# Layer 2's output projection: low weight parts formed by accumulating transfers in twelve units

## The chip, the core and the metric

The kernel runs on one core of a Trainium2 chip. The metric is the device time of the core in microseconds (us), the median of three executions: 2115.39 us for the kernel before (2115.34 to 2115.5). Beside it stands one execution taken by the hardware profiler; every duration of a single instruction below comes from that one.

## The reference

Two layers are computed over 512 tokens of width 2048 in float32: a retention layer and a layer of latent attention (16 heads of width 128). Layer 2 ends in an output projection, and that is the place of the change:

```python
o = causal_block_attention(q, k, v).reshape(B, S, MLA_WIDTH)   # 512 x 2048
return (jax.nn.silu(g) * o) @ w_out                            # w_out: 2048 x 2048
# then: x = x + gate * y, and a final rmsnorm(x, final_norm_g)
```

## The kernel before

**Precision.** A float32 matrix product is made of three products of rounded parts. Every operand `a` is held as a high part (`a` rounded to TensorE's float32r format) and a low part (`a` minus the high part). `mm3` (lines 156 to 160) issues, for one block, high times high (L158), high times low (L159) and low times high (L160), always in this order; in the projection the weights' high part is the left operand of the first two, and the weights' low part that of the third.

**The two parts of a weight.** `load_w` (L138) makes one unit of weights ready: SP (SyncE's queue of transfers) loads 128 partitions x 1024 float32 (512 KB) from HBM into a tile `raw` (three such buffers); `split` (L134) has ScalarE (ACT) copy it, rounded, into the high part (L135), and VectorE (DVE) subtract that from `raw` into the low part (L136). High and low part lie side by side in one "pair" tile. There are three pair tiles, taken in turn (`next_pair`), so a unit cannot be split before the TensorE (PE) products of the unit that held its pair before have ended.

**The output projection.** Its 2048 output rows are made in four parts of 512. The first two parts (`r` = 0 and 1 in the loop at the end of the kernel) run through `chunk`: 8 units each, every unit with 2 x 128 rows of the inner dimension. I call the units of the first part A0 to A7 and those of the second B0 to B7; in the trace all their weights are named `o_w`, their raw tiles `o_w_raw`. One unit is 24 products of 128x512 on PE. The moving operand (`o_h`, `o_l`) is the gated attention output, fetched from HBM (`o_in`<-`o_d`) and split once, and kept. Parts three and four go another way (`seven_rows_steps` with the tiles `o_00e`, `o_00o`, ...; then `last_product`), and they draw from the same pair tiles: while B7 is prepared, `seven[0]` takes one pair of the rotation for `o_00o`. So B7's pair is the one that B5 held, two units before it, where the other units' pairs were held three units before.

**Beside it.** During A0 to A3 the last two attention heads (14 and 15) are finished; POOL (GpSimd) stores their output to HBM with plain transfers (L2137, 256 KB each), and `o_in` of A7 is loaded after those stores. During B2 to B5 DVE and ACT form sums for the third part (L2416 to L2419 and L135/L136 on tiles `o_s`, `o_t`).

**Order.** Every engine works through its instructions in one fixed order, which a scheduler writes when the program is built: `queued` and `behind` keep the order of the code for the engines that they name, and elsewhere priorities decide. A wait at the head of an engine's order holds all that is behind it.

Of the kernel before, what the change touches and what calls it, by code (L numbers as in the profile page):

```python
# [9 lines left out]
F32 = mybir.dt.float32  # L10
F32R = mybir.dt.float32r
I32 = mybir.dt.int32
AF = mybir.ActivationFunctionType
ALU = mybir.AluOpType
AX = mybir.AxisListType

P = 128
T = 512
# [31 lines left out]
def hybrid_trunk_kernel(  # L50
# [25 lines left out]
    nc = tc.nc  # L76
    PE, ACT, DVE, POOL = nc.tensor, nc.scalar, nc.vector, nc.gpsimd
# [3 lines left out]
    w_mla_in, w_uq, w_ukv, w_mla_out = mla_w_in[0], mla_w_uq[0], mla_w_ukv[0], mla_w_out[0]  # L81

    base = ctx.enter_context(tc.tile_pool(name="base", bufs=1))
# [50 lines left out]
    def split(src, hi, lo):  # L134
        ACT.copy(hi, src)  # L135
        DVE.tensor_sub(lo, src, hi.bitcast(F32))  # L136

    def load_w(parts, a, b, name, later=None, where=None, halved=False):  # L138

        raw = base.tile([P, a, b], F32, tag="raw", bufs=3, name=f"{name}_raw")  # L140
        for dst, src in parts:
            nc.sync.dma_start(dst(raw), src)
        hi, lo = two_tiles(where, [P, a, b], name, ASIDE if halved else EVEN)
        if later is None:
            split(raw, hi, lo)
        else:
            later.append(lambda: split(raw, hi, lo))
        return hi, lo

    def rows(w, u, n, c0, cn):  # L150
        return w[u * n * P : (u + 1) * n * P, c0 : c0 + cn].rearrange("(k p) n -> p k n", p=P)
# [79 lines left out]
    def next_pair(name):  # L231
        i = n_pairs[0] % 3
        n_pairs[0] += 1
        return ready.pop(i, None) or pair_tile(base, f"pair{i}", name)

    def parts_of(pair, shape, at):

        n = math.prod(shape[1:])
        views = [pair[:, 1024 * i + at : 1024 * i + at + n] for i in range(2)]
        return views if len(shape) == 2 else [v.rearrange("p (k n) -> p k n", k=shape[1]) for v in views]  # L240

    def two_tiles(where, shape, name, at=EVEN):

        if where is None:
            return parts_of(next_pair(name), shape, at)
        if callable(where):
            return parts_of(where(name), shape, at)
        return [base.tile(list(shape), F32R, tag=t, bufs=n, name=f"{name}_{i}") for i, (t, n) in enumerate(where)]
# [2118 lines left out]
    def scored(pieces):  # L2367
        scores, exps, normalise = pieces[:3]
        pieces[5]()
        for i in range(NT):  # L2370
            scores(i)
            exps(i)
        normalise()
# [27 lines left out]
    def o2_parts(u):  # L2401
        o2_in[u] = k4(f"o2_in{u}", F32)
        nc.sync.dma_start(o2_in[u], o2_d[u * 2 * P : (u + 1) * 2 * P, :].rearrange("(k p) n -> p k n", p=P))
        own = k4b if u < 2 else big
        o2_hl[u] = own(f"o2_h{u}"), own(f"o2_l{u}")
        split(o2_in[u], *o2_hl[u])
# [49 lines left out]
    with behind(V_):  # L2456
        scored(last[0])

    def o2_unit(r, u):
        with ExitStack() as stack:  # L2460
            for ins in o2_first if (r, u) in ((0, 1), (0, 2)) else ():
                stack.enter_context(tc.issue_after(ins))
            wt = load_w([(whole, rows(w_mla_out, u, 2, r * T, T))], 2, T, f"o2_w{r}_{u}")
        if u not in o2_hl:
            o2_parts(u)
        return wt
# [73 lines left out]
    for r in range(2):  # L2540
        run(
            chunk(
                [(lambda u=u: o2_unit(r, u), [2 * u, 2 * u + 1]) for u in range(KD // 2)],
                [(acc, aux)[r](f"o2_{r}_{b}") for b in range(4)],
                lambda w, ki, kt, b: w_block(w, ki, b), lambda w, ki, kt, b: o2_moving(kt),
                lambda b, ps: o2_out(b, ps)() if r == 0 else waiting.append(lambda: o2_out(4 + b, ps)()),
            ),
            each=lambda i: o2_hooks(r * (KD // 2) + i),
        )
# [236 lines left out]
```

## Time and profile before

| | us |
|---|---|
| Median of three executions | 2115.39 |
| Profiled execution, its own time | 2114.73 |
| Span of its instructions | 2113.0 |
| PE busy in the span | 2098.4 (99%) |
| DVE busy | 1680.8 (80%) |
| ACT busy | 1054.1 (50%) |
| POOL busy | 103.8 (5%) |

Times of the trace count from the span's start. A0's first product stands at 1920 us, B7's last ends at 2017 us, so the change touches a stretch of about 97 us. A row of the timeline gives the start, the duration, the engine, the line, the operation, and output<-input; an entry in square brackets is idle time before it and what ended it. "Landing" of a transfer is counted from its issue. Matmuls are pipelined: their rows last 0.39 us, but they follow each other every 0.23 us.

### The profile page before, as it was taken

How to read it: one execution, taken by the hardware profiler on the slowest of the kernel's cores; microseconds unless marked ns; L12 is line 12 of the kernel's file. 1: busy time of each engine (PE TensorE's matmuls, PEld its weight loads, DVE VectorE, ACT ScalarE, POOL GpSimd, SP SyncE). 2: the span in 40 equal slices, each digit the busy share in tenths (PEclk: the TensorE clock that was granted, in tenths of full speed). 3: DMA queues.
4: the chain of work that ended last, by engine and by line, in shares of the span. 5: the costliest groups of instructions: out<-in, count | busy, mean ns of one | idle time of the engine just before them, and what ended most of it. 6: DMA issues, size and time to landing. Idle time of an engine off the chain costs nothing.

```text
span 2113.0 us, 30423 instructions
## 1 busy us (share of the span) xinstructions
PE 2098.4 (99%) x11268; PEld 1814.2 (86%) x11268; DVE 1680.8 (80%) x2562; ACT 1054.1 (50%) x1626; POOL 103.8 (5%) x177
## 2 busy tenths in 40 slices
PE   8999999999999999999999999999999999999998
PEld 6888898989889888888888888898889999888898
DVE  7999888888888789666777877767978788887675
ACT  6765444444444444434344445345446565665343
POOL 1001010000000000000000000010000000000000
PEclk9999999999999999999999999999999999999999
DMA  9975786868777778755656656753556655455453
GB/s 382 407 281 195 250 276 222 278 216 268 245 259 250 237 237 278 260 188 183 234 170 227 220 184 235 265 178 111 167 186 207 199 166 187 153 188 176 148 166 126
DMA packets 237303, 465.08 MB, mean 220 GB/s; under 512 B 21169, under 2 KB 91857, under 8 KB 233569
## 3 DMA queue, kind: packets, MB, share of 16 engines
q1 hardware_dynamic: 224512, 423.17, 60.5%
q0 software_dynamic: 11920, 38.91, 4.8%
q8 instruction: 88, 1.44, 0.3%
q10 hardware_dynamic: 722, 1.06, 0.2%
q14 instruction: 61, 0.50, 0.1%
HBM read 420.06 MB, written 43.00 MB: 219 GB/s over the span
## 4 chain that ended last, share of the span: by engine, by line
PE 95%; DMA 3%; DVE 1%; ACT 0%; SPq 0%; issue 0%; POOLq 0%; DVEq 0%
PE o L1486 16%; PE x L884 2%; PE x L883 2%; PE y L884 2%; PE y L883 2%; PE s L884 2%; PE s L883 2%; PE x L885 2%; PE s L885 2%; PE y L885 2%; PE o L2607 2%; PE qk L158 2%; PE s_qk L984 2%; PE x_qk L984 2%; PE qk L160 2%; PE qk L159 2%
## 5 line engine op out<-in xcount | busy, mean ns | idle before, releaser
L1486 PE MATMUL o<-o_h,o_p 128*128 128x512 f32 (+1 forms) x1088 | 322.9, 377 | 0.0
L1486 PEld LDWEIGHTS o<-o_h,o_p 128*128 128x128 f32 x1088 | 200.2, 188 | 37.1
L1486 PE MATMUL o<-o_l,o_p 128*128 128x512 f32 (+1 forms) x544 | 204.8, 377 | 0.0
L136 DVE TENSOR_TENSOR o_p<-o_r,o_p 128x1024 fp32r<-128x1024 f32 x64 | 78.1, 1221 | 52.5 <-ACT o_p L135 52.2
L1486 PEld LDWEIGHTS o<-o_l,o_p 128*128 128x128 f32 x544 | 102.3, 188 | 18.2
L1170 DVE SCALAR_TENSOR_TENSOR mod<-mod,c_odd 128x1024 f32<-128x1024 f32 x56 | 67.2, 1219 | 14.9 <-DMA mod<-in_ada_t_dram 14.9
L135 ACT CAST o_p<-o_r 128x1024 fp32r<-128x1024 f32 x64 | 66.7, 1053 | 21.3 <-PE o L1486 7.7
L158 PE MATMUL qk<-hT,qk_p 128*128 128x512 f32 x192 | 75.0, 391 | 0.0
L160 PE MATMUL qk<-hT,qk_p 128*128 128x512 f32 x192 | 74.8, 390 | 0.0
L159 PE MATMUL qk<-hT,qk_p 128*128 128x512 f32 x192 | 74.7, 389 | 0.0
L389 DVE SCALAR_TENSOR_TENSOR aw<-aw,c_all 128x2048 f32<-128x2048 f32 (+1 forms) x37 | 73.2, 1997 | 1.6 <-DMA aw<-in_ada_t_dram 1.4
L1332 ACT ACTIVATE yn<-y,nmr,gn_r 128x512 f32<-128x512 f32 x32 | 22.3, 777 | 67.7 <-DVE nmr L1326 67.7
L159 PE MATMUL o<-o_l,o_w 128*128 128x512 f32 x128 | 49.9, 390 | 0.3 <-DVE o_l L136 0.3
L158 PE MATMUL o<-o_h,o_w 128*128 128x512 f32 x128 | 50.1, 391 | 0.0
L160 PE MATMUL o<-o_h,o_w 128*128 128x512 f32 x128 | 49.9, 390 | 0.0
L1170 DVE SCALAR_TENSOR_TENSOR mod<-mod,c_bm 128x1024 f32<-128x1024 f32 x40 | 48.7, 1218 | 0.0
L448 PE MATMUL g<-hT,g_p 128*128 128x512 f32 x192 | 46.1, 389 | 0.0
L2046 PE MATMUL uv<-ukv_p,kvT 128*128 128x256 f32 x384 | 46.1, 279 | 0.0
L136 DVE TENSOR_TENSOR qk_p<-qk_r,qk_p 128x1024 fp32r<-128x1024 f32 x23 | 27.9, 1222 | 22.1 <-ACT qk_p L135 21.8
L2046 PEld LDWEIGHTS uv<-ukv_p,kvT 128*128 128x128 f32 x384 | 44.9, 189 | 0.1
L2607 PE MATMUL o<-o_h,o_w 128*128 128x256 f32 (+1 forms) x208 | 43.6, 306 | 0.0
L160 PEld LDWEIGHTS qk<-hT,qk_p 128*128 128x128 f32 x192 | 36.0, 188 | 7.8 <-DVE qk_p L136 0.3
(1735 smaller groups left out, 6308.0 us busy)
## 6 DMA issues: line engine op xcount, KB each, us to landing
mod<-in_ada_t_dram SPq DMA_DIRECT2D x96, 512.0 KB, 5.7
o_r<-in_ret_w_out_dram SPq DMA_DIRECT2D x64, 512.0 KB, 5.4
aw<-in_ada_t_dram SPq DMA_DIRECT2D x28, 1024.0 KB, 9.5
mod_gate<-in_ada_t_dram SPq DMA_DIRECT2D x32, 512.0 KB, 5.1
qk_r<-in_ret_w_in_dram SPq DMA_DIRECT2D x48, 256.0 KB, 3.2
qk_r<-qk_d SPq DMA_DIRECT2D x32, 256.0 KB, 5.9
v_r<-v_d SPq DMA_DIRECT2D x32, 256.0 KB, 5.8
sg<-g_d SPq DMA_DIRECT2D x32, 256.0 KB, 6.2
```

What stands on the lines that cost most here:

```text
L136: DVE.tensor_sub(lo, src, hi.bitcast(F32))
L158: PE.matmul(o, lhs[0], rhs[0], start=first and not seeded, stop=False, skip_group_check=seeded)
L159: PE.matmul(o, lhs[0], rhs[1], start=False, stop=False, skip_group_check=seeded)
L160: return PE.matmul(o, lhs[1], rhs[0], start=False, stop=last, skip_group_check=seeded)
L883: PE.matmul(banks[b], a[0], w[0], start=first, stop=False, skip_group_check=True)
L884: PE.matmul(banks[b], a[0], w[1], start=False, stop=False, skip_group_check=True)
L885: PE.matmul(banks[b], a[1], w[0], start=False, stop=True, skip_group_check=True)
L984: PE.matmul(o, w[wp][:, i, b * P : (b + 1) * P], a[ap], start=first and i + b + k == 0, stop=k == 2, skip_group_check=True,)
L1170: DVE.scalar_tensor_tensor(out=aw, in0=aw, scalar=1.0, in1=silu_c[j], op0=ALU.mult, op1=ALU.mult, accum_out=row_sums[piece][:, j, b : b + 1],)
L1486: PE.matmul(o, w[i][:, ki, c0 + b * P : c0 + (b + 1) * P], a[j], start=first and i + j == 0, stop=last and i == 1, skip_group_check=True,)
L2046: PE.matmul(ps[:, (t % 2) * 256 : (t % 2 + 1) * 256], a[i], w[k], start=t % 2 + i + k == 0 and kt == 1, stop=kt == 3 and i == 1, skip_grou ...
L2607: PE.matmul(banks3[b][:, cols], last_w[u][i][:, ki, b * P : (b + 1) * P], o2_moving(2 * u + ki, cols)[j], start=u + ki + i + j == 0, stop= ...
```

## The change

In the units with `u` > 1, six in each of the two parts, `load_w` is replaced by a new function. DVE's subtraction is gone. ACT copies the high part as before, then writes the negated high part into the low part's tile; then POOL issues a transfer that reads the same weights from HBM a second time and adds them, in the transfer, to what lies in the tile. The low part is weights minus high part again. The units A0, A1, B0 and B1 stay as they were.

```diff
+    def load_remainder(src, name):
+
+        raw = base.tile([P, 2, T], F32, tag="raw", bufs=3, name=f"{name}_raw")
+        nc.sync.dma_start(raw, src)
+        hi, lo = two_tiles(None, [P, 2, T], name)
+        ACT.copy(hi, raw)
+        ACT.activation(lo, hi.bitcast(F32), AF.Identity, scale=-1.0)
+        POOL.dma_start(lo, src, accum_op=ALU.add)
+        return hi, lo
+
     def o2_unit(r, u):
         with ExitStack() as stack:
             for ins in o2_first if (r, u) in ((0, 1), (0, 2)) else ():
                 stack.enter_context(tc.issue_after(ins))
-            wt = load_w([(whole, rows(w_mla_out, u, 2, r * T, T))], 2, T, f"o2_w{r}_{u}")
+            if u > 1:
+                wt = load_remainder(rows(w_mla_out, u, 2, r * T, T), f"o2_w{r}_{u}")
+            else:
+                wt = load_w([(whole, rows(w_mla_out, u, 2, r * T, T))], 2, T, f"o2_w{r}_{u}")
```

The raw tile is now read by ACT's copy alone, and comes free after it. PE's order of products is the same. Two places show what moves. The first is ACT's order around the last units, B5 to B7 (`o_w_5` to `o_w_7`; L2464 is the copy, L2465 the negation, L1017 and L1022 are copies for the third part; the last number of a name is a buffer's):

```order
+L2464 CAST o_w_5_18497<-o_w_5_raw 128x1024
+L135 CAST o_s_18486<-o_s7f 128x2x256
+L2465 ACTIVATE o_w_5_18497<-o_w_5_18497 128x1024
+L2464 CAST o_w_6_18541<-o_w_6_raw 128x1024
+L2465 ACTIVATE o_w_6_18541<-o_w_6_18541 128x1024
 L1017 CAST o_2_00e<-o_2_00e_r 128x1024
 L1022 CAST o_2_00o<-o_2_00o_r 128x1024
-L135 CAST o_w_7_18575<-o_w_7_raw 128x1024
+L2464 CAST o_w_7_18586<-o_w_7_raw 128x1024
+L2465 ACTIVATE o_w_7_18586<-o_w_7_18586 128x1024
 L1017 CAST o_2_01e<-o_2_01e_r 128x1024
 L1022 CAST o_2_01o<-o_2_01o_r 128x1024
```

Each unit now has two ACT instructions where it had one, the second right behind the first or one instruction later. The second place is POOL's order, from the last stores of the attention heads through A2 to A7 (`o_w_2` to `o_w_7`):

```order
 L2137 DMA o_d<-o_13_17756 128x512
-L2137 DMA o_d<-o_14_17999 128x512
-L2137 DMA o_d<-o_15_18072 128x512
+L2466 DMA o_w_2_17953<-in_mla_w_out_dram 128x2x512
+L2466 DMA o_w_3_18027<-in_mla_w_out_dram 128x2x512
+L2466 DMA o_w_4_18079<-in_mla_w_out_dram 128x2x512
+L2466 DMA o_w_5_18119<-in_mla_w_out_dram 128x2x512
+L2137 DMA o_d<-o_14_18000 128x512
+L2466 DMA o_w_6_18167<-in_mla_w_out_dram 128x2x512
+L2137 DMA o_d<-o_15_18074 128x512
+L2466 DMA o_w_7_18215<-in_mla_w_out_dram 128x2x512
```

The stores of heads 14 and 15 now stand behind the accumulating transfers of A2 to A5, and of A6.

## The prediction

> **What bounds the kernel now.** I read the page's busy times first, then who waited for whom on PE, then the stretch of B2 to B7 (B for the second part's units, A for the first's), then its rows one by one. The page:
>
> ```profile
> PE 2098.4 (99%) x11268; PEld 1814.2 (86%) x11268; DVE 1680.8 (80%) x2562; ACT 1054.1 (50%) x1626; POOL 103.8 (5%) x177
> ```
>
> PE is the bound. Next the waits of PE from 1915 to 2060 us (who <- for whom: us, times, longest), and the busy time by engine from 1970 to 2017 us, that is A7's end to B7's:
>
> ```profile
> PE o L159 <- DVE o_l L136: 0.3, 1, 0.3
> ...
> 1970.00:2017.00 47.00, 47.00 (x209) 38.92 (x208) 32.80 (x55) 18.72 (x25) 0.00 (x0) 1.00 0.46 146
> ```
>
> PE lost 0.3 us in the whole neighbourhood of the change, in A0, which the change leaves as it is; in the B units it is busy 47.00 of 47.00 us. DVE, which is relieved, ends no wait of PE there. So nothing is to be gained, and the question is whether the low parts come later than PE's L160 asks for them.
>
> **The change part by part.** Here are the weights' own rows, and two ACT groups that bear on the new negation:
>
> ```profile
> L135 ACT CAST o_w<-o_w_raw x16: 1035/1051/1057, 1885.0 to 2008.4; 128x1024 fp32r<-128x1024 f32 x16
> L136 DVE TENSOR_TENSOR o_w<-o_w_raw,o_w x16: 1209/1224/1226, 1886.1 to 2009.5; 128x1024 fp32r<-128x1024 f32 x16
> ...
> L2485 ACT ACTIVATE x<-x,vcol 128x512 f32<-128x512 f32 x4 | 2.9, 722 | 0.1
> L2484 ACT ACTIVATE x_sq<-x 128x512 f32<-128x512 f32 x3 | 1.9, 617 | 0.0
> ```
>
> Removed: 12 subtractions of 1.22 us = 14.7 us of DVE, worth 0 on PE by the waits above. Added on ACT: 12 negations of 128x1024. ACT is busy 18.72 of 47.00 us in the B stretch, so the 6 of them there fit. The copy of the same size takes 1.05 us; the scaled activation of half the size takes 0.72 against 0.62 us for an unscaled one, so the negation takes 1.05 to 1.15 us. I take 1.1.
>
> Added on POOL: 12 issues, and on the DMA engines 12 x 512 KB read from HBM once more. The trace holds no accumulating transfer. The nearest rows, in the stretch from 1915 to 2020 us (KB each, median us to landing), and the spread over all 16 loads:
>
> ```profile
> o_w_raw<-in_mla_w_out_dram SPq DMA_DIRECT2D x12, 512.0 KB, 4.0
> o_d<-o POOLq DMA_DIRECT2D x3, 256.0 KB, 3.1
> o_00e_r<-in_mla_w_out_dram SPq DMA_DIRECT2D x2, 256.0 KB, 2.9
> ...
> DMA to landing us min/median/max: 3.6/4.0/5.5
> ```
>
> A load of 512 KB takes 4.0 and one of half that 2.9, so 256 KB more cost 1.1 us. A plain POOL store of 256 KB takes 3.1; at 512 KB I make that 4.2. An accumulating transfer has also to read what lies in the tile, another 512 KB: 2 x 1.1, together 6.4 us. The low bound is the fastest plain load of the same bytes, 3.6 us; the high bound three passes of 4.0 (read, read, write), 12.0 us. I take 6.4 where the DMA engines are otherwise quiet. The Trainium skill bears on this in "Collectives: The Full Stack", Part 3, Why ReduceScatter is half of AllGather: an addition inside the transfer costs no time of its own, but its two source reads halve the rate. No row here shows it; without the second read my 6.4 would be 4.2, with it the 6.4 stands.
>
> Now where the price falls. A unit's copy starts when its pair is released, then follow negation, issue, landing. The tight one is B7, since its pair was held by B5, not by B4. PE's and ACT's rows show that:
>
> ```profile
> 2005.82 0.39 PE L160 MATMUL o<-o_h,o_w 128*128 128x512 f32 x1
> ...
> 2011.94 0.39 PE L160 MATMUL o<-o_h,o_w 128*128 128x512 f32 x1
> ...
> 2008.44 1.05 ACT L135 CAST o_w<-o_w_raw 128x1024 fp32r<-128x1024 f32 x1 [3.74 <-DMA o_w_raw<-in_mla_w_out_dram]
> 2011.73 1.05 ACT L1017 CAST o_01e<-o_01e_r 128x1024 fp32r<-128x1024 f32 x1 [2.23 <-PE o L160]
> ```
>
> The first is B5's last product, so B5 ends at 2006.21; the second is B7's first use of its low part. After B7's copy, `o_01e` takes the next pair and waits for a product that ends at about 2011.7, B6's end: so B6's pair goes to `o_01e`, and B7 has B5's. Before, B7's copy started at 2008.44 because its load landed late, not because of the pair. That load was late because of DVE:
>
> ```profile
> 2000.26 1.22 DVE L136 TENSOR_TENSOR o_w<-o_w_raw,o_w 128x1024 fp32r<-128x1024 f32 x1 [6.23 <-ACT o_w L135]
> 2001.41 0.68 DVE L1016 TENSOR_TENSOR o_00e_r<-o_00e_r 128x512 f32<-128x512 f32 x1
> ...
> 2003.46 1.22 DVE L1020 TENSOR_TENSOR o_00e<-o_00e_r,o_00e 128x1024 fp32r<-128x1024 f32 x1
> ...
> 2004.71 0.37 SPq L142 DMA_DIRECT2D o_w_raw<-in_mla_w_out_dram  x1
> ```
>
> SP issued it when L1020 freed a raw buffer, and L1016 to L1020 stood behind B6's subtraction. With the subtractions gone, and raw tiles free after the copies, this goes some us earlier: I take the load to land before 2006.2. (Would it not move, the copy would start 2.2 us later, and PE's stall be so much longer; that is an end of the range.)
>
> So B7: pair free 2006.21; copy 1.05, to 2007.3; negation 1.1, to 2008.45. From an engine's end to POOL's start, and what else POOL does:
>
> ```profile
> 1944.98 0.68 DVE L2136 TENSOR_TENSOR o<-o,sg 128x512 f32<-128x512 f32 x1
> ...
> 1945.96 0.54 POOL L2137 DMA_DIRECT2D o_d<-o  x1 [27.51 <-DVE o L2136]
> 1953.74 0.54 POOL L2137 DMA_DIRECT2D o_d<-o  x1 [7.24 <-DVE o L2136]
> ```
>
> 0.3 us: POOL starts at 2008.75. Other transfers are under way here:
>
> ```profile
> 2008.00:2013.00 5.00, 5.00 (x24) 4.14 (x23) 3.40 (x5) 2.11 (x2) 0.00 (x0) 1.00 0.51 159
> ```
>
> The DMA engines were half busy (0.51) with weights of the third part, and the next of those loads waits for the raw tile that B7's copy frees at 2007.3, so 512 KB run beside the accumulation. Sharing costs up to 2.2 us (2 x 1.1), perhaps nothing; I take the half, 1.1. Landing: 6.4 + 1.1 = 7.5, at 2016.25. PE wants it at 2011.94: **a stall of 4.3 us**, and 0.1 for refilling PE.
>
> The other units have room. B2 is the tightest: its pair comes free with A7's end, 1973.18 + 0.39 = 1973.57.
>
> ```profile
> 1973.18 0.39 PE L160 MATMUL o<-o_h,o_w 128*128 128x512 f32 x1
> 1984.74 0.39 PE L160 MATMUL o<-o_h,o_w 128*128 128x512 f32 x1
> ...
> 1974.27 1.04 ACT L135 CAST o_w<-o_w_raw 128x1024 fp32r<-128x1024 f32 x1
> 1975.21 0.71 ACT L2485 ACTIVATE x<-x,vcol 128x512 f32<-128x512 f32 x1
> 1975.84 0.62 ACT L2484 ACTIVATE x_sq<-x 128x512 f32<-128x512 f32 x1
> ```
>
> Two activations stand between copy and negation, so this ends at 1976.46 + 1.1 = 1977.6, POOL starts at 1977.9, and PE wants the part at 1984.74: room for 6.8, against 6.4. A7 has more:
>
> ```profile
> 1957.29 1.05 ACT L135 CAST o_w<-o_w_raw 128x1024 fp32r<-128x1024 f32 x1 [5.79 <-PE o L160]
> 1960.61 1.05 ACT L135 CAST o_h<-o_in 128x1024 fp32r<-128x1024 f32 x1 [2.26 <-DMA o_in<-o_d]
> ...
> 1967.97 0.39 PE L158 MATMUL o<-o_h,o_w 128*128 128x512 f32 x1
> 1968.42 0.39 PE L160 MATMUL o<-o_h,o_w 128*128 128x512 f32 x1
> ```
>
> Copy from 1957.29, POOL at 1959.75, wanted at 1968.42: 8.7. The stores of heads 14 and 15, now behind accumulations on POOL, hold up nobody: A6's accumulation is ready at about 1953.0, before the store at 1953.74, and were the store late, `o_h`, copied at 1960.61, is first used at 1967.97, over 5 us of cover after copy and subtraction.
>
> The sum: 0 (DVE) + 0 (ACT, other units) + 4.4 (B7) = +4.4 us on the profiled execution's 2114.73, its span of 2113.0 and 1.73 around it. That execution lies 0.66 below the median, so I add to the median: 2115.39 + 4.4 = **2119.8 us**.
>
> **The rivals.**
>
> *The accumulation is fast.* It lands like a plain transfer: 3.6 to 6 us at B7, stall 0.4 to 2.8 us, at the middle 4.8 us: +1.6 and 0.1, 2117.1 us. For it: transfers of 512 KB land within 5.5 here, and the DMA engines are half idle. Against it: the tile has to be read too. It is not slower by what can be told, and that holds for all landings under 7.2 us at B7.
>
> *The accumulation is slow everywhere,* 9 us and more. Then B2 stalls too, from 6.8 us on, and B5, whose pair is B2's, and B7 whose pair is B5's:
>
> ```profile
> 1989.50 0.39 PE L160 MATMUL o<-o_h,o_w 128*128 128x512 f32 x1
> 2001.06 0.39 PE L160 MATMUL o<-o_h,o_w 128*128 128x512 f32 x1
> ```
>
> B2 ends at 1989.89; copy, a cast of 0.6 and negation bring B5's POOL start to 1992.9; room 8.1. With 9 us: 2.2 (B2) + 0.9 (B5) + 5.8 (B7) + A7's 0.3 = 9.2, 2124.6 us. With 12 us: about 5.2 + 3.8 + 8.8 + 3.3 in A6 and A7 = 21, 2136.5 us. For it: nothing in this kernel accumulates in a transfer, so no row limits the price. Against: two reads need not cost more than two reads.
>
> *The stall lowers PE's clock.* At the end of the program PE ends at 2105.88, and the granted clock (third column from the right) halves by 2110:
>
> ```profile
> 2102.19 3.69 PE L2715 MATMUL y_ps<-ident,x 128*128 128x128 f32 x32
> ...
> 2105.00:2110.00 5.00, 0.88 (x9) 0.65 (x6) 1.79 (x3) 0.98 (x2) 0.00 (x0) 1.00 1.04 369
> 2110.00:2113.00 3.00, 0.00 (x0) 0.00 (x0) 0.00 (x0) 0.00 (x0) 0.00 (x0) 0.50 0.33 84
> ```
>
> So some 4.1 us without work were enough there, and B7's stall is 4.3. If half clock lasts as long again, 4.1 us do the work of 2.05: 4.4 + 2.05 = 6.5, 2121.8 us. The Trainium skill ("TensorE: Matmul & The Clock Gate", Part 1) has the clock halved after one idle window of about 3.4 us and restored after as long a busy one, the windows running freely; by that a stall of 4.3 meets a whole idle window only if it lies well. The one drop here agrees with it.
>
> *A gain:* something earlier by freed DVE time that PE was waiting for. The waits show 0.3 us in all, so no more than that.
>
> **How the numbers follow.** Forecast, one stall at B7, landing there in 6 to 9 us: 0.47, time +2.9 to +6, or +8 where B2 joins. Fast: 0.21. Slow: 0.22. Clock: 0.08. Gain or other: 0.02. A measurement of this kernel tells 0.2% (4.2 us) from no change, which B7's landing reaches at 7.2 us; of the forecast's 0.47 I give 0.22 to landings under it. Same: 0.21 + 0.22 = 0.43. Slower: 0.25 + 0.22 + 0.08 = 0.55. Faster: 0.02. The range: low at the fast bound, +0.5 at 3.6 us, 2115.9; high well into the slow case, about 10.5 us, some +15, 2131.
>
> **What would show it.** PE's waits should have one new row, L160 for the transfer into `o_w`, once, 3 to 6 us long, at about 2012; two or three such waits speak for the slow case, none over 2 us for the fast one. The landing of the accumulating transfers should be 6 to 8 us. B7's copy should start at 2006.2 to 2006.4, ended by PE, and not by its load; else the raw buffers did not come earlier. ACT's negation should read 1.05 to 1.15 us. The granted clock should stay at 1.00 through 2005 to 2020. Wrong altogether: no wait of PE and less than 2114 us, or waits of PE outside L160.

## The result and the profile after

The changed kernel takes 2126.41 us (median of four runs, 2126.07 to 2127.3) against 2115.36 before: 11.05 us more, a ratio of 1.0053 with a 95% interval of 1.0036 to 1.0071. The forecast was 2119.8 us, +4.4. It is slower, as forecast, and inside the stated range (2115.9 to 2131), but the loss is two and a half times the forecast's. The profiled execution has a span of 2124.7 us (2113.0 before).

The busy times of the page, then PE's waits from 1915 to 2075 us (who <- for whom: us, times, longest), after the change:

```profile
PE 2102.7 (99%) x11268; PEld 1816.5 (85%) x11268; DVE 1668.2 (79%) x2550; ACT 1065.2 (50%) x1638; POOL 118.4 (6%) x189
...
PE o L160 <- DMA o_w<-in_mla_w_out_dram: 7.9, 4, 4.9
```

DVE has lost 12.6 us, ACT gained 11.1 and POOL 14.6, and PE, which had no such wait, waits four times for the accumulated low parts. Where they stand in PE's timeline (start, us, ..., idle time before it and what ended it):

```profile
1969.11 0.50 PE L160 MATMUL o<-o_h,o_w 128*128 128x512 f32 x1 [0.23 <-DMA o_w<-in_mla_w_out_dram]
...
1993.10 0.50 PE L160 MATMUL o<-o_h,o_w 128*128 128x512 f32 x1 [1.94 <-DMA o_w<-in_mla_w_out_dram]
...
2010.61 0.50 PE L160 MATMUL o<-o_h,o_w 128*128 128x512 f32 x1 [0.88 <-DMA o_w<-in_mla_w_out_dram]
...
2021.20 0.79 PE L160 MATMUL o<-o_h,o_w 128*128 128x512 f32 x1 [4.86 <-DMA o_w<-in_mla_w_out_dram]
```

These are A7, B3, B6 and B7. Behind the last, a matmul takes 0.79 instead of 0.50 us. The windows view around it has the granted clock third from the right (us, then busy time of PE, PEld, DVE, ACT, POOL; then clock, share of the DMA engines, GB/s):

```profile
2016.29:2019.70 3.41, 0.06 (x1) 0.00 (x0) 1.23 (x1) 0.69 (x1) 0.28 (x1) 1.00 0.84 143
2019.70:2023.12 3.42, 1.92 (x5) 1.53 (x6) 0.00 (x0) 0.00 (x0) 0.00 (x0) 0.50 0.30 55
2023.12:2026.53 3.41, 3.41 (x10) 2.63 (x9) 0.00 (x0) 0.00 (x0) 0.00 (x0) 0.50 0.00 0
```

PE ran at half clock for 6.83 us, of which it was busy 1.92 + 3.41 = 5.33: half of that, 2.7 us, is lost. I compared the start of each unit in the two traces: A7 came out 0.5 us longer than before, B3 2.3, B6 1.2, and B7 7.6 (4.86 of wait, 2.7 of half clock). With 0.3 us that the program was already late at A1, this is 11.9, the end of PE's last instruction less the end of the one before (11.8).

### The profile page after: what moved, and what is told of

Same layout as the page of the kernel before. It is cut to its first block, busy times and chain, and to the rows that moved or that the text cites. A ratio compares the mean times of both kernels' runs of the same rounds, so it can differ in the third digit from the quotient of the medians.

```text
span 2124.7 us, 30452 instructions
## 1 busy us (share of the span) xinstructions
PE 2102.7 (99%) x11268; PEld 1816.5 (85%) x11268; DVE 1668.2 (79%) x2550; ACT 1065.2 (50%) x1638; POOL 118.4 (6%) x189
## 3 DMA queue, kind: packets, MB, share of 16 engines
q8 instruction: 88, 1.44, 0.3%
q10 hardware_dynamic: 722, 1.06, 0.2%
## 4 chain that ended last, share of the span: by engine, by line
PE 93%; DMA 4%; issue 1%; DVE 1%; ACT 1%; SPq 0%; POOLq 0%; POOL 0%; DVEq 0%; ACTq 0%
PE o L1486 16%; PE x L884 2%; PE x L883 2%; PE s L884 2%; PE y L884 2%; PE x L885 2%; PE y L883 2%; PE s L883 2%; PE y L885 2%; PE s L885 2%; PE qk L158 2%; PE s_qk L984 2%; PE x_qk L984 2%; PE qk L160 2%; PE qk L159 2%; PE y_qk L984 2%
```

## Why the waits are there

The groups of the weights' instructions after the change (duration in ns min/median/max), and the spread of the accumulations' landings:

```profile
L2464 ACT CAST o_w<-o_w_raw x12: 1032/1050/1057, 1921.9 to 2012.9; 128x1024 fp32r<-128x1024 f32 x12
L2465 ACT ACTIVATE o_w<-o_w x12: 1045/1060/1084, 1923.8 to 2013.9; 128x1024 fp32r<-128x1024 f32 x12
L2466 POOL DMA_DIRECT2D o_w<-in_mla_w_out_dram x12: 1172/1203/1268, 1925.2 to 2015.4; - x12
...
DMA to landing us min/median/max: 5.8/7.6/10.8
```

With little beside it an accumulation lands in 5.8 us (B2, B7), beside other transfers in up to 10.8; B3's took 10.2, from 1982.9 to 1993.06. Next the share of the DMA engines (second number from the right) in the stretch of B2 to B6. It is the sum of the packets' times over the time of all 16 engines, and since packets' times can overlap it can pass 1. First before the change:

```profile
1980.00:1990.00 10.00, 10.00 (x46) 8.29 (x45) 10.00 (x22) 4.49 (x8) 0.00 (x0) 1.00 0.18 49
1990.00:2002.00 12.00, 12.00 (x55) 9.93 (x54) 5.02 (x9) 2.62 (x3) 0.00 (x0) 1.00 0.66 223
```

and after it:

```profile
1980.00:1990.00 10.00, 10.00 (x46) 8.29 (x45) 8.59 (x21) 6.53 (x9) 2.44 (x2) 1.00 1.01 241
1990.00:2002.00 12.00, 10.06 (x45) 8.00 (x44) 4.11 (x8) 2.52 (x3) 1.20 (x1) 1.00 0.95 238
```

The engines went from a share of 0.18 and 0.66 to about 1, for 22 us on end. By queue, from 1978 to 2003 us (packets, MB, share of the 16 engines; q0 carries POOL's transfers, q1 SP's), before the change:

```profile
q1 hardware_dynamic: 2784, 3.70, 45.4%
```

and after it:

```profile
q0 software_dynamic: 1088, 2.10, 48.6%
q1 hardware_dynamic: 2378, 3.30, 39.1%
```

Four accumulations were 2.10 MB and took 48.6% of 25 us, 12.2 us of all 16 engines: 3.0 us each. That is not a product of the crowding: with little beside it B7's took even more, 56.8% of the 6 us from 2015.3 to 2021.3, that is 3.4 us:

```profile
q0 software_dynamic: 272, 0.52, 56.8%
```

SP's loads, which had 45.4% of the engines' time from 1978 to 2003 us before, have to share them. What this did to the loads is in the timeline. SP's issue of B6's raw weights before the change, and ACT's copy of them on their arrival:

```profile
1993.45 0.38 SPq L142 DMA_DIRECT2D o_w_raw<-in_mla_w_out_dram  x1
...
1999.18 1.05 ACT L135 CAST o_w<-o_w_raw 128x1024 fp32r<-128x1024 f32 x1 [6.49 <-DMA o_w_raw<-in_mla_w_out_dram]
```

After the change, SP's issues of B6's and B7's raw weights, and ACT's and DVE's work on what follows:

```profile
1991.82 0.38 SPq L2462 DMA_DIRECT2D o_w_raw<-in_mla_w_out_dram  x1
...
2006.46 0.37 SPq L2462 DMA_DIRECT2D o_w_raw<-in_mla_w_out_dram  x1
...
2002.09 1.05 ACT L2464 CAST o_w<-o_w_raw 128x1024 fp32r<-128x1024 f32 x1 [8.82 <-DMA o_w_raw<-in_mla_w_out_dram]
2003.18 1.06 ACT L2465 ACTIVATE o_w<-o_w 128x1024 fp32r<-128x1024 f32 x1
2004.14 1.03 ACT L1017 CAST o_00e<-o_00e_r 128x1024 fp32r<-128x1024 f32 x1
...
2012.86 1.05 ACT L2464 CAST o_w<-o_w_raw 128x1024 fp32r<-128x1024 f32 x1 [6.73 <-DMA o_w_raw<-in_mla_w_out_dram]
...
2005.21 1.23 DVE L1020 TENSOR_TENSOR o_00e<-o_00e_r,o_00e 128x1024 fp32r<-128x1024 f32 x1 [10.11 <-ACT o_00e L1017]
```

B6's load is issued at 1991.82 and B6's copy starts, on its arrival, only at 2002.09: 10.3 us, where it was 5.7 us from issue to copy before the change. Behind it on ACT stands L1017 (`o_00e`), behind that DVE's L1020, and behind that B7's load: issued at 2006.46, copied at 2012.86. So the chain that the forecast expected to shorten (DVE's subtractions gone) had become longer by its load: DVE idled 10.11 us ahead of L1020.

My theory for the experiments: the accumulations occupy the DMA engines, make each other (B3) and SP's queue of loads (B6, and by the chain B7) late, and B7's wait also halves PE's clock. The rivals: ACT's added negation makes the loss; the price is the second reading from HBM, not the addition; raw tiles that come free early bunch SP's loads; the low parts are simply wanted too early.

## The experiments

Differences are medians against the kernel before on the same chip; every ratio has its 95% interval.

| run | us | less before | ratio, interval | PE's waits (us) |
|---|---|---|---|---|
| A2 to A7 only | 2115.29 | +0.3 | 1.0002 [0.9992, 1.0011] | none |
| B2 to B7 only | 2127.0 | +12.0 | 1.0057 [1.0042, 1.0072] | B3 3.6, B7 5.8 |
| all but B7 | 2120.09 | +5.1 | 1.0026 [1.0016, 1.0035] | B3 2.1, three under 0.8 |
| low products last | 2126.78 | +11.8 | 1.0056 [1.0041, 1.0071] | B7 4.8, five of 0.4 to 1.0 |
| plain second load | 2119.3 | +4.2 | 1.0021 [1.0012, 1.0031] | B3 1.3, B7 1.8 |
| DVE adds | 2118.11 | +3.0 | 1.0013 [1.0004, 1.0022] | B7 0.4 and 1.6 |
| B7 only | 2122.27 | +7.2 | 1.0034 [1.0022, 1.0046] | B7 5.8 |
| raw tile read by DVE too | 2128.37 | +13.3 | 1.0065 [1.005, 1.008] | B2 0.9, B3 3.6, B7 4.0 |
| added from SBUF | 2132.51 | +17.3 | 1.0085 [1.0068, 1.0101] | B5 2.0, B6 5.5, B7 3.7 |
| subtraction kept | 2133.74 | +18.6 | 1.0089 [1.0074, 1.0104] | A7 0.8, B5 2.8, B6 4.1, B7 2.8 |
| rows later | 2123.26 | +8.1 | 1.0039 [1.0024, 1.0054] | B3 1.0, B7 4.7 |
| rows earlier | 2121.41 | +6.2 | 1.003 [1.0017, 1.0042] | B3 0.6, B7 3.1, A7 1.0 |

### Which units: the first part, the second, all but B7, B7 alone

Each of the four added lines stands in a kernel of its own:

```diff
-            if u > 1:
+            if u > 1 and r == 0:          # the first part only
+            if u > 1 and r == 1:          # the second part only
+            if u > 1 and (r, u) != (1, 7):  # all but B7
+            if (r, u) == (1, 7):          # B7 only
```

> Accumulating transfers only in A2 to A7; the second part's units keep DVE's subtraction. Theory (contention and B7's late load): the loss is made in the B units, so A alone costs only A7's short wait, +0.2 to +0.5 us, and PE's waits show L160 for a transfer into o_w at most once, under 0.5 us. Rival (the accumulation is dear in itself, in every unit alike): about half of the +11, +4 to +6 us.

> Accumulating transfers only in B2 to B7. Contention and B7's late load: nearly the whole loss, +9 to +11 us, waits of PE in B3, B6 and B7 (about 2, 1 and 5 us), and the halved clock behind B7's. Rival (every unit costs alike): +4 to +6 us. Rival (the transfers of the first part shift the loads that the second part meets): clearly less than +9.

> As the change, but B7 keeps DVE's subtraction. If B7's wait of 4.9 us and the half clock behind it (about 2.7 us) are B7's own, 7.6 us go and +3 to +4 remain: A7's 0.2, B3's 1.9, B6's 0.9. Its copy still starts late if B6's late load is what holds up the loads behind it, since L1017 and B7's load come after B6's copy; with DVE's 1.2 us behind the copy B7's low part would be ready at about 2015, and some 1 to 3 us of wait on DVE instead of the transfer would remain (+4 to +7).

> The accumulating transfer in B7 alone. Theory that B7's wait comes from its raw load, which stands behind the third part's split on DVE whatever the other units do: copy at 2008.4, POOL at 2010.9, landing in 5.8 to 6.5, so a wait of 4.8 to 5.5 us and a stretch of half clock (1.7 to 3.4 us): +6.5 to +9 us. Theory that B7's lateness is made by the other units' transfers (B6's load late, and B7's behind it): the wait is as in the theory before less the 4.4 us by which B7's copy was later in the change (2012.9 against 2008.4), that is under 1 us and no half clock: +0 to +1 us.

The first part alone costs nothing, although its accumulations land no faster:

```profile
DMA to landing us min/median/max: 5.8/7.7/9.9
```

With landings of 5.8 to 9.9 us PE does not wait once. So neither the accumulation as such nor the two stores behind it on POOL is the loss; it is made in B2 to B7, where the whole of it comes back (+12.0). There the waits are not quite those expected: B3's is longer (3.6 us, with half clock behind it) and B6 has none. The profiled execution is the longest of the four (2129.78 us against the median of 2127.0).

Without B7's accumulation +5.1 are left, and its profile explains them mostly by B3. PE's row in the timeline:

```profile
1994.20 0.70 PE L160 MATMUL o<-o_h,o_w 128*128 128x512 f32 x1 [2.06 <-DMA o_w<-in_mla_w_out_dram]
```

and the windows around it, PE's busy time second and the clock third from the right:

```profile
1990.92:1994.33 3.41, 1.35 (x7) 0.81 (x6) 2.49 (x7) 2.52 (x3) 0.00 (x0) 1.00 1.10 277
1994.33:1997.74 3.41, 3.41 (x9) 2.63 (x10) 1.67 (x3) 0.00 (x0) 1.18 (x1) 0.50 1.10 254
```

A wait of 2.06 us was enough for 3.41 us of half clock, another 1.7 us. By the units' starts B3 came out 4.0 us longer than before, A6 and A7 together 1.6 (PE waits there 1.1 us for `o_h` and `o_l`), B6 0.5. B7 itself does not wait.

B7 alone costs +7.2. Its rows on ACT and PE in the timeline:

```profile
2009.06 1.05 ACT L2464 CAST o_w<-o_w_raw 128x1024 fp32r<-128x1024 f32 x1 [4.05 <-DMA o_w_raw<-in_mla_w_out_dram]
...
2018.03 0.80 PE L160 MATMUL o<-o_h,o_w 128*128 128x512 f32 x1 [5.76 <-DMA o_w<-in_mla_w_out_dram]
```

The theory that only the other units make B7 late (+0 to +1) falls: here nothing else accumulates, and B7's load still ends its wait at 2009.06, since L1020 comes behind B6's subtraction on DVE as before the change. That is the case "the load does not move" of the forecast. B7's step has thus two ways to be late, DVE's work where the subtractions stay and a late B6 load where they go; in the change it was the second. The two parts (+7.2 and +5.1) add up to 12.3, near the +11.05 of the whole; since B7 is late by another way in each of the two kernels, the sum does not prove that the shares are independent.

### Is the low part only wanted too early? All high products first

In the units from the third on, the last of each part among them, PE does the 16 products with the weights' high part first (L175 and L176 there) and the 8 with the low part last (L178). The main lines of the edit:

```diff
+            if lows_last and ui > 1:
+                for part in range(2):
+                    for ki, b in steps:
+                        emit_part(part, w, kts, ki, b, False, False)
 ...
```

> As the change, but in the units of the two parts (from the third unit on, and in the last unit of each part) PE does all 16 products with the weights' high part first and the 8 with the low part after them, so that the low part is wanted some 3.6 us later. If the loss is idle time of PE ahead of the low part, B3's and B6's waits go, B7's shrinks from 4.9 to about 1.3 us, the clock is not halved, and the time is +1 to +3 us. If the clock halves for a reason other than the wait, it does so here too, and +4 or more remain. If the loss is contention on loads (the high parts late too), the waits move to L158 and the sum stays.

It gained nothing (+11.8). ACT's rows of B6 and B7 in its timeline, and PE's wait in B7:

```profile
2006.68 1.05 ACT L2487 CAST o_w<-o_w_raw 128x1024 fp32r<-128x1024 f32 x1 [9.22 <-DMA o_w_raw<-in_mla_w_out_dram]
...
2016.68 1.05 ACT L2487 CAST o_w<-o_w_raw 128x1024 fp32r<-128x1024 f32 x1 [5.97 <-DMA o_w_raw<-in_mla_w_out_dram]
...
2026.48 3.78 PE L178 MATMUL o<-o_h,o_w 128*128 128x512 f32 x8 [4.78 <-DMA o_w<-in_mla_w_out_dram]
```

PE had 3.9 us of high products in B7 ahead of the wait, against 0.6 us in the change, and still waited 4.8 us: measured from B7's first product, the transfer landed 3.2 us later than in the change. B6's load, issued at 1994.6, took 12 us instead of 10, and both copies wait for their loads. PE also waited for `o_h` and `o_l` in A7 (1.0 and 0.8 us), as it did in three kernels with the old order, and this execution was already 0.8 us later at A0; from B0 on it runs 2.8 us behind the change's. Of the expected outcomes it is the last, contention on loads, though the waits on high products are small (0.4 us in B7). A low part that is wanted later does not help where the load of the raw weights is late; how much of the later landing is this order's own, the run does not separate.

### What the transfer is: plain, from SBUF, none

```diff
-        POOL.dma_start(lo, src, accum_op=ALU.add)
+        POOL.dma_start(lo, src)                          # plain second load
+        DVE.tensor_add(lo, raw, lo.bitcast(F32))         # DVE adds
+        POOL.dma_start(lo, raw, accum_op=ALU.add)        # added from SBUF
```

> As the change, but the second transfer only writes the weights over the negated high parts and adds nothing: the low part is then the whole weight instead of the remainder (a part of the computation is changed, the number and order of instructions and transfers is not). If the addition inside the transfer (the tile read, and written again) is the price, the transfers land in 4 to 6 us instead of 5.8 to 10.8, B3 does not wait, B6's load is not late, and the time is +0 to +4 us. If the second reading of the weights from HBM is the price, landings stay at 7 us and more beside the third part's loads, and +7 to +11 us remain.

> As the change, but DVE adds the raw weights to the negated high parts, and there is no second transfer. If the transfers make the loss, it is gone: -0.5 to +1 us, no wait for o_w over 0.3 us. If ACT's added negation and the longer chain of a unit make it, +3 us or more remain, with waits of PE for DVE in B3 and B7.

> As the change, but the accumulating transfer reads the weights from their raw tile in SBUF, not from HBM a second time; the raw tile is then held until the transfer has read it. If the engines of the transfers are the bound (each accumulation occupies all 16 for some 3.0 us by the change's queue, 48.6% of 25 us for four, against 1.7 us for a plain transfer), the landings and the loss stay: landing 6 quiet and 8 to 11 beside loads, +8 to +12 us. If reading HBM twice is what costs, landings fall to about 5 and the time to +0 to +5 us.

The plain second load keeps every byte read from HBM, leaves out the addition, and leaves +4.2 of the +11.05: near the first of the two outcomes expected, though B3 still waits 1.3 us. The spread of its landings:

```profile
DMA to landing us min/median/max: 4.3/5.3/8.8
```

and its queues from 1978 to 2003 us:

```profile
q1 hardware_dynamic: 2809, 3.73, 45.8%
q0 software_dynamic: 1311, 2.54, 34.8%
```

Per MB the plain transfer occupies the 16 engines for 0.348 x 25 / 2.54 = 3.4 us, the accumulating one for 0.486 x 25 / 2.10 = 5.8 us, 1.7 times as much. The Trainium skill ("Collectives: The Full Stack", Part 3, Why ReduceScatter is half of AllGather) puts a collective that adds at half the rate of one that copies, by its two reads; these runs of a kernel's own transfer agree in direction, with 1.7 in occupation and 5.8 against 4.3 us in quiet landing. Here B7 goes as the forecast's steps had it:

```profile
2007.81 1.05 ACT L2464 CAST o_w<-o_w_raw 128x1024 fp32r<-128x1024 f32 x1 [4.39 <-PE o L160]
...
2010.26 0.72 POOL L2466 DMA_DIRECT2D o_w<-in_mla_w_out_dram  x1 [10.17 <-ACT o_w L2465]
...
2015.43 0.50 PE L160 MATMUL o<-o_h,o_w 128*128 128x512 f32 x1 [1.76 <-DMA o_w<-in_mla_w_out_dram]
```

The copy is released by PE's last product of B5, POOL starts 2.45 us behind it (forecast 2.54), and PE waits once there, without a drop of the clock.

With no second transfer at all (DVE adds) +3.0 are left, more than the theory that transfers make the whole loss allowed. PE's row in B7:

```profile
2014.70 0.50 PE L160 MATMUL o<-o_h,o_w 128*128 128x512 f32 x1 [1.61 <-DVE o_w L2466]
```

and the windows around it:

```profile
2012.00:2015.41 3.41, 1.45 (x5) 0.93 (x6) 1.96 (x3) 1.44 (x3) 0.00 (x0) 1.00 0.04 14
2015.41:2018.83 3.42, 3.42 (x10) 2.65 (x9) 2.39 (x3) 0.96 (x1) 0.00 (x0) 0.50 0.55 155
```

The negation makes every unit's chain 1.06 us longer. B6's copy starts 1.4 us later than before (2000.57 for 1999.18), its sum on DVE another 1.1 us, and DVE's order carries that on through L1020 to B7's load, which was issued at 2007.19 instead of 2004.71. B7 then waits 0.4 us for its copy and 1.6 us for its sum, and half clock doubles that. So the rival of the negation holds for a part: the length of the chain has a price of its own of about 3 us where B7's load hangs on it. It does not simply add to the transfers' share, since in the change L1020 was held up by B6's load and not by DVE.

Added from SBUF, HBM is read once, and a quiet transfer lands in 4.5 us; but the raw tile is held until the transfer has read it, the next loads start later, and the loss grows to +17.3, outside both ranges expected. The engines are nearly as occupied as with HBM (from 1978 to 2003 us):

```profile
q0 software_dynamic: 572, 2.10, 44.6%
```

That is 5.3 us per MB against 5.8, and 3.4 without the addition. So the second reading from HBM is not the main price of the engines' time; the addition is. That it costs by a second read of the tile fits, but no run takes the read apart from the sum. This run has two edits in one (the source, and how long a raw tile is held), so the +17.3 itself is not split.

### Are the loads bunched? The raw tile held longer

```diff
         POOL.dma_start(lo, src, accum_op=ALU.add)
+        DVE.tensor_copy(small(f"{name}_k"), raw[:, 0, 0:1])   # raw tile read by DVE too
```

```diff
+        DVE.tensor_sub(raw, raw, hi.bitcast(F32))             # subtraction kept, result unused
         POOL.dma_start(lo, src, accum_op=ALU.add)
```

> As the change, but a DVE copy of one column of the raw tile keeps that tile occupied until DVE comes to it, so that SP's loads behind it (the next units' and the third part's) are not issued earlier than before the change. If bunched loads make the contention, B3's transfer lands in under 8.5 us instead of 10.2 and it does not wait, B6's copy starts near 1999 to 2000 instead of 2002.1, and the time is +4 to +8 us, B7's wait being what is left. If the accumulating transfers' own traffic is enough for it, B3's wait of 2 us and the whole +10 to +12 us stay.

> As the change, but DVE's subtraction is still done, into the raw tile itself, where nobody uses the result: raw tiles come free as late as before the change, and DVE has its old work, so the loads of SP should be issued near the times of before (B5's at about 1987 instead of 1981.3, B6's at about 1993). If the earlier bunch of loads makes the loss, B3's transfer lands in about 6 us, no wait there, and what is left is B7's: +6 to +9 us, as where B7 alone accumulates (+7.2). If the transfers' own occupation of the engines is enough, B3 or a later unit waits for 2 us and more, B6's load still takes 8 us or more, and the loss is +10 us or more.

The first did not do what it was meant to: DVE came to the small copy early, and B5's load was issued at 1983.4, not at 1987 as before. It decides nothing. The second did: B5's and B6's loads went out at 1988.9 and 1996.9 (before the change 1987.0 and 1993.5). SP's row of B6 and ACT's copy of B6:

```profile
1996.90 0.38 SPq L2462 DMA_DIRECT2D o_w_raw<-in_mla_w_out_dram  x1
...
2006.61 1.05 ACT L2464 CAST o_w<-o_w_raw 128x1024 fp32r<-128x1024 f32 x1 [9.51 <-DMA o_w_raw<-in_mla_w_out_dram]
```

The load still took nearly 10 us, and the loss rose to +18.6. For B3 the early loads did matter: with B5's and the third part's loads issued from 1988.9 on, behind B3's accumulation (1985.2), and not from 1981.3 on, ahead of it, that accumulation landed in 6.2 us instead of 10.2, and PE did not wait there. For B6 and B7 the early issue was not the cause: their loads take as long when they are issued late, beside accumulations, and only start later. The waits moved to B5, B6 and B7. With DVE's work kept, POOL also waited for DVE in B6, by some 0.2 us, which is a small part of it.

### Other traffic moved: the rows of the residual later, and earlier

Four loads of residual rows (`o_xr`, 1 MB together) stood in SP's queue ahead of B6's weights. One kernel issues them behind the third part's loads, another ahead of the first of these:

```diff
-                if i == 14:
+        if i == 15:                       # rows later
+                if i == 13:               # rows earlier, ahead of seven[0]'s loads
                     for kt in range(4, 8):
                         o2_residual(kt)
```

> As the change, but the four loads of residual rows (o_xr, 256 KB each), which stood ahead of B6's and B7's weights in SP's queue, are issued behind the third part's first loads. If B6's and B7's late loads come from the queue and the engines being full, B6's copy starts some 3 us earlier (near 1999), B7's by 2 to 4 us (2009 to 2011), B7's wait is 1 to 3 us instead of 4.9, without a half clock or with a short one: +3 to +6 us in all, B3's wait staying or shorter. If the queue does not matter, nothing changes: +10 to +12 us.

> As the change, but the four loads of residual rows (o_xr, 1 MB together) are issued before the third part's first loads, at about 1971, where the engines of the transfers are half idle, and so out of the way of B3 to B7. If the engines' occupation by loads and accumulations together makes the loss, all of B3's to B6's waits go or stay under 1 us, B6's and B7's loads land in about 5, B7's copy is released by PE (B5's end) at 2006.2 to 2007.5, its transfer lands in about 6, and one wait of 3.3 to 4.5 us at about 2012 is left, with or without a stretch of half clock: +3.5 to +7 us, the case that was forecast. If the rows do not matter, B7's wait stays behind a late load and the loss is +8 to +11 us.

With the rows later, the loss is +8.1: B3 waits 1.0 instead of 1.9, B6 0.15, and B6's copy starts at 1996.56 instead of 2002.09. But the rows now load beside B7's accumulation:

```profile
2008.65 1.05 ACT L2464 CAST o_w<-o_w_raw 128x1024 fp32r<-128x1024 f32 x1 [5.60 <-DMA o_w_raw<-in_mla_w_out_dram]
...
2018.49 0.79 PE L160 MATMUL o<-o_h,o_w 128*128 128x512 f32 x1 [4.71 <-DMA o_w<-in_mla_w_out_dram]
```

B7's transfer was issued at 2011.17 and took 7.3 us, its load 7.6: the contention went where the rows went. My numbers for B7's wait (1 to 3 us) and for the loss (+3 to +6) missed that.

With the rows earlier, the loss is +6.2, and what is left at B7 is the forecast's own case. B7's rows:

```profile
2009.51 1.05 ACT L2464 CAST o_w<-o_w_raw 128x1024 fp32r<-128x1024 f32 x1 [4.39 <-PE o L160]
...
2012.02 1.20 POOL L2466 DMA_DIRECT2D o_w<-in_mla_w_out_dram  x1 [9.53 <-ACT o_w L2465]
...
2018.49 0.50 PE L160 MATMUL o<-o_h,o_w 128*128 128x512 f32 x1 [3.12 <-DMA o_w<-in_mla_w_out_dram]
```

The copy is released by PE, as B5 ends (at 2009.5 and not 2006.2, since PE is 3.3 us late by then); POOL follows 2.5 us later; the transfer lands 6.4 us after its issue; PE waits 3.1 us, and 3.41 us of half clock follow. By the units' starts B7 came out 5.0 us longer than before the change, B3 0.9, and A6 and A7 together 1.6, where PE waits for `o_h` and `o_l`. The accumulations are all there, as in the change, and those of B3 to B5 still take 7.9 to 8.8 us; the engines, too, are still full (shares of 1.08 from 1980 to 1990 us and 0.94 to 2002). What has changed is the queue: 1 MB less stands ahead of B6's load, which now takes 5.4 us instead of 10, and B7's chain is no longer held up by it. So it is the loads' backlog on full engines that made B6 and B7 late, not a long accumulation at B7.

No kernel here is faster than the one before: even without any wait (the first part alone) the difference is +0.3 us with an interval on both sides of none, since PE was busy throughout.

## Why the prediction was right or wrong

**Nothing to gain: right.** PE waited 0.3 us before, and no run that took work from DVE became faster.

**The negation: right in its price, 1.06 us against 1.1,** wrong in its cost of nothing. With DVE in place of the transfer, the longer chain alone cost +3.0.

**The landing: the quiet price a little too high** (5.8 us against 6.4; B7's own was 5.8 against 7.5). Its two terms can be told apart: a plain transfer of 512 KB on POOL's queue lands in 4.3 us where I made it 4.2, and the addition costs 1.5 us more where I took 2.2. The bounds of 3.6 and 12.0 held all twelve. What failed is that I gave the sharing to B7 alone, as 1.1 us: beside loads the price went up to 10.8 us.

**"The other units have room": this step failed.** B3 was never worked out by itself; I took B2 for the tightest, and by room it was (7.5 us from POOL's start to PE's first use in the changed kernel, B3 8.3). But I put one quiet price against every room. B2 landed in 5.8 us, while B3's transfer met B5's load, the third part's and the rows, took 10.2, and made 1.9 us of wait. A count from the profile before could have warned me: SP's loads alone took 45.4% of the engines from 1978 to 2003 us, and three or four transfers of double traffic beside them fill the rest. I costed the duration of a transfer and not its occupation of the engines that others need.

**B7's load "goes earlier", copy at 2006.2 by PE: this step failed,** and its bound (2.2 us later) too. The copy came at 2012.86, 4.4 us later than before the change, since B6's load took 10.3 us on full engines and B7's load hangs on it by ACT, L1020 and the raw buffer. I freed that chain of DVE's subtractions and did not ask what the added transfers do to its load. Where B6's load is not held up (the plain load, the rows earlier) the step holds: copy released by PE, POOL 2.5 us behind it.

**B7's stall: 4.86 us against 4.3.** The size is near by cancellation: a start 6.6 us late (2012.86 for 2006.21), a landing 1.7 us short, and PE itself 4.2 us late at B7.

**The clock: the rival came true as well,** with 2.7 us instead of 2.05. I gave it 0.08, since a stall of 4.3 us seemed to need luck; in the runs a 2 us wait could do it.

**The sum:** forecast +4.4, all at B7. In the profile: B7 7.6, of which 2.7 are clock; B3 2.3; B6 1.2; A7 0.5. The rival of accumulations "slow everywhere" gave +9.2, near the total, but by landings of 9 us in every unit, which is not what happened: the first part, with landings up to 9.9, lost nothing. That the time lies in the stated range is luck in the same way: its upper part stood for that rival, and neither B6's late load nor its way to B7 was among the forecast's terms.

**The stores of heads 14 and 15: nothing in the change, as said, but with less cover than I counted.** Head 15's store lands in 5.7 us behind A6's accumulation (3.1 before), so `o_in` is issued at 1959.52 instead of 1956.89; over 5 us of cover took that. In four other kernels (all but B7, low products last, subtraction kept, rows earlier) the store and the load behind it were later still, and PE waited 0.8 to 1.8 us in A7 for `o_h` and `o_l`.

**What stays open:** how the +17.3 with the source in SBUF and the +18.6 with the subtraction kept divide among their edits; and why the runs of kernels with long waits spread more (2119.5 to 2125.1 with the rows earlier, 2114.8 to 2115.6 before beside it). That a wait falls differently into the clock's windows from run to run would fit, but was not measured.

## What to carry to other kernels

Cost an added transfer twice: by how long it takes alone, and by how long it occupies the DMA engines in the stretch where it runs, beside what the profile already shows there; if the sum of shares reaches one, loads queue up behind each other there, and the work that hangs on the last of them decides. Where PE is the bound and waits for no other engine, work taken from another engine is worth nothing, and each wait on PE of about 2 us and more can cost half as much again, or double, by the clock. A step that "goes earlier" must be followed back to the load that starts it, under the changed traffic.

## What the runs showed of the hardware

**The clock halves after less idle time than I thought, and by windows.** All stretches of half clock in these profiles ahead of the program's last windows, 16 in 11 kernels, lasted 3.41 or 6.83 us, and where one kernel had several, they began a whole number of 3.41 us apart. Laid on that grid, a window with 1.96 us or more of PE idle was followed by half clock; one with up to 1.69 us was not (1.44 in the kernel of the plain second load, 1.69 at the end of the kernel of the first part alone). The change's B3 wait (1.94 us) fell across two windows and cost no clock:

```profile
1988.98:1992.39 3.41, 2.19 (x10) 1.49 (x8) 2.26 (x7) 1.93 (x4) 0.46 (x1) 1.00 1.09 267
1992.39:1995.81 3.42, 2.71 (x12) 2.23 (x13) 2.64 (x4) 0.88 (x1) 1.20 (x1) 1.00 1.12 275
```

The wait of 2.06 us in the kernel without B7, inside one window (PE busy 1.35 of 3.41 us), cost 3.41 us of half clock, and so did the 1.6 and 0.4 us of the kernel in which DVE adds (busy 1.45). Full speed came back after a window with at most 0.5 us idle; a window with 1.3 us or more kept the half clock for another. The Trainium skill ("TensorE: Matmul & The Clock Gate", Part 1) has the clock set by free-running windows of 3413 ns, halved after an idle window; the grid agrees, but here the window need not be idle throughout, 57% of it was enough.

**An accumulating transfer of 512 KB** lands in 5.8 us with little beside it (a plain one on the same queue in 4.3), keeps POOL for 1.2 us at its issue (a plain one 0.7), and its packets take 3.0 us of all 16 engines, where a plain one's take 1.8.
